# Forming the second round's block sums beside the first output projection, in a two-layer decoder trunk

## The chip, the cores and the metric

The kernel runs on one core of one Trainium2 chip. The metric is the device time of one execution in microseconds (us); a lower time is better. The engines are named as in the profile: PE (matmuls) with PEld (its weight loads), DVE (vector), ACT (activations), POOL (general) and SP, the queue from which this kernel issues its DMAs.

## The reference

Two layers over one sequence of 2048 rows with 1024 columns, all in float32. Layer 0 is called even in the code, layer 1 odd. Only this much bears on the change:

```
def even_layer(x, g_norm, w_in, b_f, g_q, g_k, w_out):
    h = rmsnorm(x, g_norm)
    proj = h @ w_in
    ...
    return x + mixed @ w_out

def odd_layer(x, g_norm, w_in, g_q, g_k, w_out):
    h = rmsnorm(x, g_norm)
    proj = h @ w_in
    q, k, v, gate = jnp.split(proj, split_points(ODD_SIZES), axis=-1)
    ...
    return x + mixed @ w_out
```

The input projection of the odd layer multiplies 2048 x 1024 by 1024 x 5120. Its left operand is the normalised output of the even layer, which comes out of the even layer's output projection.

## The kernel before, in words

**Products by seven.** Each input projection is done in two rounds of 1024 rows. In a round the left operand is cut into two by two blocks of 512 rows by 512 columns, 11 12 over 21 22, and each panel of 512 weight columns is computed with seven block products instead of eight. The left operands are four blocks taken as they are or as sums: A11, A12, S1 = 21 + 22, S2 = S1 - 11, S3 = 11 - 21, A22 = 22, S4 = 12 - S2. The weights' sums are formed the same way by `Weights.prepare` (POOL's line L226 does the sums, then ACT L81 and POOL or DVE L86 split each into a rounded part and a rest). Every product is three matmuls of the rounded parts and rests (`mm3`, L91 to L93), so one block product is 48 matmuls of 128x256, and a panel 336. `panel_steps` runs a panel in the order of `ORDER`; `two` opens two panels at once, with A11 and A12 of both ahead of S2, S3, S1, A22 and S4 of each. DVE adds the partial results (L300) and ACT copies them (L305).

**Where the left operands come from.** In the odd layer `left` makes them. The transposed, normalised rows lie in a DRAM scratch `T` (`hT` in the profile). `left` loads pieces of 128x512 (`lp`, L362), forms the sums on DVE and POOL (helper `tt`, L345) and splits each into its two parts (`put`: ACT L81, DVE L86) into one of eight large buffers. For the first round (`staged=True`) blocks 11 and 12 are loaded once into a buffer `stage`, and the pieces take six small buffers (tags `ld`, `q`, `pT`, two each). For the second round (`staged=False`) no room is left for `stage`: the blocks 11 and 12 are rebuilt from the two parts of the operands already made, and the pieces share the four buffers of tag `c` with other work. Here are the sums that this costs:

```
            for h in half(A[A11], kk):
                tt(s, s, h, sub)
...
            hi, lo = half(A[A12], kk)
            h2, l2 = half(A[S2], kk)
            tt(s, hi, h2, sub)
            tt(s, s, lo, plus)
            tt(s, s, l2, sub)
```

In the even layer the second round is prepared otherwise: `combined_to` makes all seven blocks ahead of time, 128 rows at a time, into a scratch `U`, and `left_ready` only loads and splits.

**The order of the work.** `first_out` is the even layer's output projection: 16 tiles of 128 rows (`rows`), staggered, so that in step s tile s is loaded, tile s-1 multiplied, added to x, stored and normalised, and tile s-2 transposed (L142) and stored to `T`. In steps 13 and 14 it also starts `left` for the first round. Then come the odd layer's panels: first round q and k of group 1 through `two`, then v, then the other groups, then the gate panel. While the gate panel runs, a call after each of its seven products (`after=lambda j: next(nxt)`) moves the second round's `left` one step on, since each product frees one large buffer. Attention units run between the panels' half products. The program is written in this order, but a scheduler may move instructions ahead on an engine when they are ready; each engine and the SP queue then run their instructions strictly in the order they got. All DMAs that matter here are on SP.

Of the kernel before, what the change touches and what calls it, by code (L numbers as in the profile page):

```python
# [8 lines left out]
F32 = mybir.dt.float32  # L9
# [3 lines left out]
OP = mybir.AluOpType  # L13
# [4 lines left out]
P = 128  # L18
S = 2048
D = 1024  # L20
KT = D // P
CH = 512
# [14 lines left out]
class K:  # L37
# [114 lines left out]

    def transpose_to(self, T, src, t, gain):

# [6 lines left out]
        self.transposed(x, gain, lambda z: self.c2([P, 4, P], name="te"),  # L161
                        lambda z, d: nc.sync.dma_start(T[:, z * 4:(z + 1) * 4, t * P:(t + 1) * P], d))

# [12 lines left out]
A11, A12, S2, S3, S1, A22, S4 = range(7)  # L176
# [164 lines left out]

def left(k, T, r, A, staged=True):

# [15 lines left out]
    def piece(block, kk):  # L359
        c = k.c2(name="lp", tag=next(tags))  # L360
        t0 = r * ROUND + block * CH
        nc.sync.dma_start(c, T[:, kk, t0:t0 + CH])  # L362
        return c
# [94 lines left out]
def left_ready(k, U, A, tags):  # L458

    A.extend([None] * 7)  # L460
    tags = itertools.cycle(tags)
    for j in FIRST:
        t = A[j] = k.big([P, 4, 2, CH], F32R, name=f"A{j}")
        for kk in range(4):
            c = k.c2(name="lp", tag=next(tags))
            k.nc.sync.dma_start(c, U[:, j, kk])
            k.split(t[:, kk, 0], t[:, kk, 1], c, "act", "dve")
        yield
# [525 lines left out]
        tail()  # L994


def first_out(k, x, x1, w, T, W, lefts):

    nc = k.nc
    wo, raws, ml = {}, {}, {}
    quarters = [(n, z) for n in range(2) for z in range(2)]

    def load(i):
        n, z = quarters[i]
        raws[i] = [k.raws.tile([P, 2, CH], F32, name="wraw", tag="raw") for _ in range(2)]
        for j, raw in enumerate(raws[i]):  # L1010
            k0 = (z * 4 + j * 2) * P
            nc.sync.dma_start(raw, w[k0:k0 + 2 * P, n * CH:(n + 1) * CH].rearrange("(k p) n -> p k n", p=P))

    def quarter(i):
        t = wo[quarters[i]] = k.big([P, 4, 2, CH], F32R, name="wo")
        for j, raw in enumerate(raws.pop(i)):
            k.split(t[:, 2 * j:2 * j + 2, 0], t[:, 2 * j:2 * j + 2, 1], raw, "act", "dve")

    def mixed(b):
        t = ml[b] = k.big([P, KT, 2, 2 * P], F32R, name="ml")  # L1020
        for j in range(4):
            c = k.c2([P, 2, 2 * P], name="mp", tag="res")
            nc.sync.dma_start(c, k.mixT[:, 2 * j:2 * j + 2, b * 2 * P:(b + 1) * 2 * P])
            k.split(t[:, 2 * j:2 * j + 2, 0], t[:, 2 * j:2 * j + 2, 1], c, "act", "dve")

    def rows(t):
        xt = k.w4([P, D], name="xt")
        nc.sync.dma_start(xt, x[t * P:(t + 1) * P, :])
        yield
        m, i = ml[t // 2], slice(t % 2 * P, (t % 2 + 1) * P)  # L1030
        for n in range(2):
            acc = k.ps("s")
            for kk in range(KT):
                k.mm3(acc, [m[:, kk, z, i] for z in range(2)],
                      [wo[n, kk // 4][:, kk % 4, z] for z in range(2)], kk == 0, kk == KT - 1)
            half = xt[:, n * CH:(n + 1) * CH]
            nc.vector.tensor_tensor(half, acc, half, op=OP.add)
        nc.sync.dma_start(x1[t * P:(t + 1) * P, :], xt)
        k.normalise(xt)
        yield  # L1040
        k.transposed(xt, k.go, lambda z: k.c2([P, 4, P], name="te"),
                     lambda z, d: nc.sync.dma_start(T[:, z * 4:(z + 1) * 4, t * P:(t + 1) * P], d))

    load(0)
    load(1)
    for i in range(4):
        yield
        quarter(i)
        if i < 2:
            load(i + 2)  # L1050
    steps = staggered(rows(t) for t in range(NTT))
    for b in range(2):
        yield
        mixed(b)
    yield
    for s in range(NTT + 2):
        next(steps, None)

        if s in (2, 4, 6, 8, 10, 12):
            mixed(s // 2 + 1)  # L1060
        if s == 9:
            W.ahead(1)
        if s in (13, 14):
            next(lefts)


def odd_layer(k, x, x1, even_w_out, w_in, w_out, out):
    tc, nc = k.tc, k.nc
    c2, dr = k.c2, k.dram
    T = dr.tile([P, KT, S], F32, name="hT1")  # L1070
    plain = lambda c0: [[(c0, 256)], [(c0 + 256, 256)]]
    rounds = [[(n, g) for g in gs for n in "qkv"] + [("gate", 0)] for gs in ((1, 0, 2), (2, 1, 0))]
    cols = lambda n, g: plain(3 * 1536 if n == "gate" else "qkv".index(n) * 1536 + g * 512)
    W = Weights(k, [(w_in, cols(*j)) for js in rounds for j in js], [2, 1, 1, 1, 1, 1, 1, 1, 1] * 2)
    A = []
    lefts = left(k, T, 0, A)
    yield from first_out(k, x, x1, even_w_out, T, W, lefts)
    tick = Pace()
    tick.add(lefts)

# [195 lines left out]

    for r in range(2):
        B = []
        nxt = left(k, T, 1, B, False)
        for i, (name, grp) in enumerate(rounds[r]):  # L1280
            rate = 3 if r == 0 or i < 3 else 1.3
            count = [0.0]

            def beat():
                tick()
                count[0] += 1
                if count[0] >= rate:
                    count[0] -= rate
                    step()

            last = r == 0 and name == "gate"
            if i < 2:
                if i == 0:
                    both = two(A, [emitter(r, *rounds[r][n]) for n in range(2)], beat)
                    next(both)
                    if r == 0:
                        tick.finish()

                        box = k.big([P, 4, HG, 2, P], F32R, name="box")
                        bias = box[:, 0].bitcast(F32)  # L1300
                        values = [box[:, 3].bitcast(F32).rearrange("p a b c -> p (a b c)")[:, i * HW:(i + 1) * HW] for i in range(4)]
                        values += [k.hs.tile([P, HW], F32, name=f"v{i}") for i in range(2)]
                        ring = box[:, 1:3].rearrange("p x a b c -> p (x a b c)").rearrange("p (z h s t) -> p z h s t", z=2, h=2, s=4)
                        pairs = box[:, 1:3].rearrange("p x a b c -> p (x a b c)").rearrange("p (z s h e t) -> p z s h e t", z=2, s=2, h=2, e=2)
                next(both)
            else:
                panel(k, A, W, "t", emitter(r, name, grp), beat, (lambda j: next(nxt)) if last else None)
            if name == "v":
                nblk = S // GROUPS[grp][1] // P
                if nblk == 1:  # L1310
                    if r == 1:
                        queue.extend((True, attention(grp, hf, range(16), range(1))) for hf in range(2))
                else:
                    ns = range(r * nblk // 2, (r + 1) * nblk // 2)
                    queue.extend((False, attention(grp, hf, range(GROUPS[grp][1]), ns)) for hf in range(2))
        A = B
    ws = []
    for n in range(2):
        t = k.big([P, 4, 2, CH], F32R, name="wof")
# [120 lines left out]
```

## Time and profile before

| what | value |
|---|---|
| median of 3 runs | 2769.3 us (2765.4 to 2769.72) |
| the profiled execution | 2767.75 us, of which its span 2766.0 us |
| mean granted PE clock | 0.991 |
| busy: PE, PEld, DVE, ACT, POOL | 96%, 87%, 70%, 57%, 40% of the span |
| first output projection, last tile's matmuls end | about 1477 us |
| first round of the odd layer begins | 1475 us |
| second round of the odd layer begins | 1986 us |

How to read it: matmuls overlap, so a busy PE is not yet a PE at its pace. Better is to count matmuls in a stretch and to compare with a stretch that runs undisturbed; the views by window give both, and the clock that was granted. Lines are those of the kernel before.

### The profile page before, as it was taken

To read this page: it belongs to the slowest core of one execution; us is meant where nothing else is said; L and a number is where in the kernel's file an instruction comes from. 1 tells how busy PE (TensorE), PEld (TensorE's weight loads), DVE (VectorE), ACT (ScalarE), POOL (GpSimd) and SP (SyncE) were. 2 spreads that over 40 slices of the span, in tenths; PEclk is the share of its full clock that TensorE was granted. 3 is DMA by queue.
4 is the path that set the end of the run, shared out by engine and by line. 5 is a ranking of instruction groups with operands and counts; after the bars stand their busy time and mean duration, and the time that the engine had idled before them with its cause. 6 is when DMAs were issued, how large, how long until landed. Compare 5 with 4: busy or idle time off the path is not lost.

```text
span 2766.0 us, 54039 instructions
## 1 busy us (share of the span) xinstructions
PE 2664.9 (96%) x19615; PEld 2418.7 (87%) x19615; DVE 1923.3 (70%) x4255; ACT 1577.2 (57%) x3843; POOL 1102.5 (40%) x903
## 2 busy tenths in 40 slices
PE   6999999999998899999999899999989999999998
PEld 5899878998787789988889899999889999999876
DVE  7867774684788887787237767475896676663976
ACT  6456654454767665665546345555663678665642
POOL 3545654544544433332004654343254432422322
PEclk9999999999999999999999999999999999999999
DMA  5576864445433334443564333444634444444675
GB/s 184 179 214 186 276 209 146 153 143 190 151 115 117 118 116 145 142 132 111 193 203 149 111 108 116 131 133 128 203 98 143 129 154 146 141 138 141 222 257 184
DMA packets 382154, 432.56 MB, mean 156 GB/s; under 512 B 30976, under 2 KB 315968, under 8 KB 381888
## 3 DMA queue, kind: packets, MB, share of 16 engines
q1 hardware_dynamic: 381888, 429.11, 48.3%
q8 instruction: 155, 2.54, 0.4%
q14 instruction: 111, 0.91, 0.1%
HBM read 271.30 MB, written 157.71 MB: 155 GB/s over the span
## 4 chain that ended last, share of the span: by engine, by line
PE 70%; DVE 17%; ACT 5%; DMA 3%; issue 3%; POOL 1%; SPq 1%; DVEq 0%; ACTq 0%; POOLq 0%
PE ps L91 19%; PE ps L93 19%; PE ps L92 19%; DVE rest L893 4%; PE ps L928 3%; PE ps L1237 2%; PE ps L1227 2%; PE ps L1208 2%; PE ps L1153 1%; DVE pT L86 1%; DVE wop L86 1%; DVE c L300 1%; DVE row L1214 1%; PE ps L1200 1%; DVE lp L345 1%
## 5 line engine op out<-in xcount | busy, mean ns | idle before, releaser
L226 POOL TENSOR_TENSOR wraw<-wraw 128x512 f32<-128x512 f32 (+1 forms) x288 | 396.7, 1388 | 417.2 <-DVE wop L86 158.0
L91 PE MATMUL ps<-wop,A 128*128 128x256 f32 (+1 forms) x1856 | 528.5, 285 | 3.8 <-DVE c L300 3.8
L92 PE MATMUL ps<-wop,A 128*128 128x256 f32 (+1 forms) x1856 | 527.2, 284 | 0.0
L93 PE MATMUL ps<-wop,A 128*128 128x256 f32 (+1 forms) x1856 | 525.5, 283 | 0.0
L81 ACT ACTIVATE wop<-wraw 128x512 fp32r<-128x512 f32 (+1 forms) x504 | 315.4, 628 | 339.6 <-PE ps L93 266.0
L86 POOL TENSOR_TENSOR wop<-wraw,wop 128x512 fp32r<-128x512 f32 (+1 forms) x216 | 291.2, 1351 | 494.4 <-ACT wop L81 479.5
L86 DVE TENSOR_TENSOR wop<-wraw,wop 128x512 fp32r<-128x512 f32 (+1 forms) x288 | 234.1, 814 | 239.8 <-ACT wop L81 237.6
L91 PE MATMUL ps<-wop,S 128*128 128x256 f32 x1280 | 369.8, 289 | 4.5 <-DVE c L300 4.5
L92 PE MATMUL ps<-wop,S 128*128 128x256 f32 x1280 | 364.1, 284 | 2.4 <-DVE wop L86 2.4
L93 PE MATMUL ps<-wop,S 128*128 128x256 f32 x1280 | 365.6, 286 | 0.0
L91 PEld LDWEIGHTS ps<-wop,A 128*128 128x128 f32 x1856 | 351.9, 190 | 8.1 <-DVE c L300 4.6
L93 PEld LDWEIGHTS ps<-wop,A 128*128 128x128 f32 x1856 | 352.3, 190 | 1.2 <-issue 0.7
L92 PEld LDWEIGHTS ps<-wop,A 128*128 128x128 f32 x1856 | 352.0, 190 | 0.7 <-issue 0.5
L91 PEld LDWEIGHTS ps<-wop,S 128*128 128x128 f32 x1280 | 242.6, 190 | 8.8 <-issue 8.0
L92 PEld LDWEIGHTS ps<-wop,S 128*128 128x128 f32 x1280 | 243.1, 190 | 4.2 <-DVE wop L86 2.6
L93 PEld LDWEIGHTS ps<-wop,S 128*128 128x128 f32 x1280 | 242.8, 190 | 3.4 <-issue 2.7
L81 ACT ACTIVATE pT<-ps 128x512 fp32r<-128x512 f32 (+2 forms) x352 | 164.7, 502 | 136.8 <-PE ps L928 93.4
L300 DVE TENSOR_TENSOR c<-u,ps 128x512 f32<-128x512 f32 (+1 forms) x242 | 157.4, 656 | 90.3 <-PE ps L93 84.6
L86 DVE TENSOR_TENSOR pT<-ps,pT 128x512 fp32r<-128x512 f32 (+2 forms) x352 | 187.7, 559 | 43.8 <-ACT pT L81 42.3
L896 POOL TENSOR_TENSOR rows<-rows,rest 128x512 f32<-128x512 f32 (+4 forms) x160 | 152.4, 956 | 160.3 <-DVE rest L893 153.1
L1220 ACT ACTIVATE row<-row,nm 128x256 f32<-128x256 f32 (+1 forms) x384 | 172.4, 451 | 64.2 <-DVE nm L1218 60.6
L93 PE MATMUL ps<-A,wop 128*128 128x512 f32 x448 | 177.2, 397 | 4.4 <-DVE ms L104 4.4
(222 smaller groups left out, 6778.3 us busy)
## 6 DMA issues: line engine op xcount, KB each, us to landing
wraw<-in_odd_w_in_dram SPq DMA_DIRECT2D x88, 512.0 KB, 4.0
wraw<-in_even_w_in_dram SPq DMA_DIRECT2D x70, 512.0 KB, 4.2
ld<-qk SPq DMA_DIRECT2D x106, 256.0 KB, 3.1
qk<-c SPq DMA_DIRECT2D x96, 256.0 KB, 2.5
uu<-ot SPq DMA_DIRECT2D x96, 132.0 KB, 1.9
fin<-uu SPq DMA_DIRECT2D x16, 792.0 KB, 4.7
xt<-in_x_dram SPq DMA_DIRECT2D x24, 512.0 KB, 4.5
vv<-c SPq DMA_DIRECT2D x48, 256.0 KB, 2.5
```

The source lines that it names most:

```text
L81: nc.scalar.activation(hi, src, AF.Copy)
L86: (nc.vector if lo_on == "dve" else nc.gpsimd).tensor_tensor(lo, src, hi.bitcast(F32), op=OP.subtract)
L91: mm(out, a[0], b[0], start=start, stop=False, skip_group_check=more)
L92: mm(out, a[0], b[1], start=False, stop=False, skip_group_check=more)
L93: mm(out, a[1], b[0], start=False, stop=stop, skip_group_check=more)
L226: tt = lambda e, o, x, y, op, s: e.tensor_tensor(o[:, s], x[:, s], y[:, s], op=op)
L300: nc.vector.tensor_tensor(out[g], x[g], y[g], op=OP.add)
L893: nc.vector.tensor_tensor_scan(o[:, b:b + n][:, ::-1], back, k.ident[:, :1].to_broadcast([P, n]), 1.0 if carry is None else carry, OP.mult ...
L896: nc.gpsimd.tensor_tensor(dst[:, :w], dst[:, :w], o[:, b + 1:b + 1 + w], op=OP.mult)
L928: nc.tensor.transpose(pt[:, (jx * 2 + i) * P:(jx * 2 + i + 1) * P], rows[:, i, (jj * 2 + jx) * P:(jj * 2 + jx + 1) * P], k.ident)
L1208: nc.tensor.matmul(scores(hp, e), q[pr, za, hp], ring[pr, zb, hp, blocks], start=i == 0, stop=i == 2)
L1220: nc.scalar.activation(row[:, h // 2, h % 2, :nk], row[:, h // 2, h % 2, :nk], AF.Exp, bias=nm[:, h:h + 1], accum_out=ot[:, HW + HG + h:HW ...
```

## The change

The second round's seven blocks are no longer made from `T` during the gate panel. They are made in `first_out`, as the even layer does it, from the tiles as they are transposed: tiles 8 to 11 hold the upper blocks 11 and 12 and go to the new scratch `U` as they are. For each tile 12 to 15 the matching upper blocks are loaded back (`above`, two DMAs, tag `res`), and A22, S1, S2, S3 and S4 are formed and stored: two operations on POOL, two on DVE, five stores. In the gate panel `left_ready` loads and splits what lies in `U`. `T` shrinks to the first round's rows. The first round still uses `left` with `stage`, in the same steps 13 and 14.

```
@@ first_out, rows(t)
         xt = k.w4([P, D], name="xt")
         nc.sync.dma_start(xt, x[t * P:(t + 1) * P, :])
+        at = slice(t % 4 * P, (t % 4 + 1) * P)
+        if t >= 12:
+            a = [k.c2([P, 4, P], name="above", tag="res") for _ in range(2)]
+            for z in range(2):
+                nc.sync.dma_start(a[z], U[:, (A11, A12)[z], :, at])
         yield
...
-        k.transposed(xt, k.go, lambda z: k.c2([P, 4, P], name="te"),
-                     lambda z, d: nc.sync.dma_start(T[:, z * 4:(z + 1) * 4, t * P:(t + 1) * P], d))
+        if t < 8:
+            k.transposed(xt, k.go, lambda z: k.c2([P, 4, P], name="te"),
+                         lambda z, d: nc.sync.dma_start(T[:, z * 4:(z + 1) * 4, t * P:(t + 1) * P], d))
+            return
+
+        def store(j, d):
+            nc.sync.dma_start(U[:, j, :, at], d)
+
+        if t < 12:
+            k.transposed(xt, k.go, lambda z: k.c2([P, 4, P], name="te"), lambda z, d: store((A11, A12)[z], d))
+            return
+        b = [k.c2([P, 4, P], name="te") for _ in range(2)]
+        k.transposed(xt, k.go, lambda z: b[z])
+        store(A22, b[1])
+        s1, s2, s4 = (k.c2([P, 4, P], name="lp", tag=n) for n in ("ld", "q", "pT"))
+        nc.gpsimd.tensor_tensor(s1, b[0], b[1], op=OP.add)
+        store(S1, s1)
+        nc.vector.tensor_tensor(s2, s1, a[0], op=OP.subtract)
+        store(S2, s2)
+        nc.gpsimd.tensor_tensor(b[0], a[0], b[0], op=OP.subtract)
+        store(S3, b[0])
+        nc.vector.tensor_tensor(s4, a[1], s2, op=OP.subtract)
+        store(S4, s4)
@@ odd_layer
-    T = dr.tile([P, KT, S], F32, name="hT1")
+    T = dr.tile([P, KT, S // 2], F32, name="hT1")
+    U = dr.tile([P, 7, 4, CH], F32, name="hU1")
...
-        nxt = left(k, T, 1, B, False)
+        nxt = left_ready(k, U, B, ("c",))
```

The tiles `s1`, `s2` and `s4` take the buffers of tags `ld`, `q` and `pT`, which the first round's pieces `lp` take as well. So the scheduler places the first round's work anew. The instructions of all engines keep their order elsewhere; they move in two places: from the last tiles of `first_out` into the first two panels, and beside the gate panel.

**The SP queue at the end of `first_out`.** Before, a piece is `lp<-hT`, the transposed rows `hT<-te`, a panel's weights `wraw`, the first results `qk<-c`:

```order
L1038 DMA x1d<-xt 128x1024
L1042 DMA hT_7557<-te 128x4x128 x2
L362 DMA lp<-hT_7557 128x512 x5
L1038 DMA x1d<-xt 128x1024
L362 DMA lp<-hT_7557 128x512
L1042 DMA hT_7557<-te 128x4x128
L1134 DMA box<-biases 128x1024
L1042 DMA hT_7557<-te 128x4x128
L216 DMA wraw<-in_odd_w_in_dram 128x4x256 x2
L1042 DMA hT_7557<-te 128x4x128 x2
L216 DMA wraw<-in_odd_w_in_dram 128x4x256
L1121 DMA qk_16985<-c 128x2x256 x2
```

These were the last six of the sixteen pieces. In the changed kernel the same place, from the last store of tile 14 on, reads as follows (L1054 is a store to `U`; `te` is a transposed tile or S3, `lp` one of S1, S2, S4):

```order
L216 DMA wraw<-in_odd_w_in_dram 128x4x256
L1054 DMA hU_7558<-te 128x4x128
L362 DMA lp<-hT_7557 128x512
L1054 DMA hU_7558<-lp 128x4x128
L362 DMA lp<-hT_7557 128x512
L1054 DMA hU_7558<-lp 128x4x128
L362 DMA lp<-hT_7557 128x512
L1054 DMA hU_7558<-lp 128x4x128
L362 DMA lp<-hT_7557 128x512
L216 DMA wraw<-in_odd_w_in_dram 128x4x256
L362 DMA lp<-hT_7557 128x512
L1054 DMA hU_7558<-te 128x4x128
```

All sixteen pieces now stand behind the transposed tile 15, the first of them directly behind its A22 store; the seventh to ninth stand behind the first results `qk<-c`, and the last four behind all results of both opened panels' first products.

**DVE at the same place.** Before, the splits of S2 (`S_17027`), S3 (`S_17095`), S1 (`S_17164`) stand between the last two tiles' additions (L1037):

```order
L112 TENSOR_SCALAR t<-t 128x1
L86 TENSOR_TENSOR S_17027<-lp,S_17027 128x512
L114 TENSOR_TENSOR r_16844<-r,t 128x1
L86 TENSOR_TENSOR S_17027<-lp,S_17027 128x512 x2
L1037 TENSOR_TENSOR xt<-ps,xt 128x512
L86 TENSOR_TENSOR S_17027<-lp,S_17027 128x512
L86 TENSOR_TENSOR S_17095<-stage,S_17095 128x512 x4
L345 TENSOR_TENSOR lp<-lp 128x512
L86 TENSOR_TENSOR S_17164<-lp,S_17164 128x512 x2
L1037 TENSOR_TENSOR xt<-ps,xt 128x512
```

In the changed kernel they come after the first normalised result (L1146, which was L1117), and S2 (`S_17084`) and S3 (`S_17152`) are made slice by slice between the panels' own work:

```order
L1146 TENSOR_TENSOR c<-c,r_17280 128x512 x2
L345 TENSOR_TENSOR lp<-lp 128x512
L86 TENSOR_TENSOR wop<-wraw,wop 128x2x256
L345 TENSOR_TENSOR lp<-lp,stage 128x512
L345 TENSOR_TENSOR stage<-stage,lp 128x512
L300 TENSOR_TENSOR c<-u,ps 128x512
L86 TENSOR_TENSOR S_17084<-lp,S_17084 128x512
L300 TENSOR_TENSOR c<-u,ps 128x512
L86 TENSOR_TENSOR S_17152<-stage,S_17152 128x512
L124 TENSOR_REDUCE ss<-sq 128x8
L345 TENSOR_TENSOR lp<-lp,stage 128x512
```

All forming and splitting of S2, S3, S1, A22 and S4 moved from ahead of the last tile's addition to behind the first opened panel's first result. The fourth slice of S2 is split 22 rows after the first, the fourth of S1 another 17 rows on.

**DVE beside the end of the gate panel.** Before, at S4 of the second round (`S_23812`; `A_23154` is A12, `S_23296` is S2; L1109 and L1113 belong to the gate's results):

```order
L1109 TENSOR_SCALAR e<-c 128x512
L345 TENSOR_TENSOR lp<-A_23154,S_23296 128x512
L345 TENSOR_TENSOR lp<-lp,A_23154 128x512
L345 TENSOR_TENSOR lp<-lp,S_23296 128x512
L1113 TENSOR_TENSOR c<-c,e 128x512
L345 TENSOR_TENSOR lp<-A_23154,S_23296 128x512
L345 TENSOR_TENSOR lp<-lp,A_23154 128x512
L86 TENSOR_TENSOR S_23700<-lp,S_23700 128x512
L86 TENSOR_TENSOR S_23812<-lp,S_23812 128x512
L345 TENSOR_TENSOR lp<-lp,S_23296 128x512
L86 TENSOR_TENSOR wop<-wraw,wop 128x2x256
L345 TENSOR_TENSOR lp<-A_23154,S_23296 128x512
```

In the changed kernel, at S4 (`A_23837`; `A_23746` is A22, L1138 and L1142 are the gate's lines):

```order
L300 TENSOR_TENSOR c<-u_23006,ps 128x512 x2
L86 TENSOR_TENSOR A_23746<-lp,A_23746 128x512 x2
L86 TENSOR_TENSOR wop<-wraw,wop 128x2x256
L1142 TENSOR_TENSOR c<-c,e 128x512
L86 TENSOR_TENSOR A_23837<-lp,A_23837 128x512
L1142 TENSOR_TENSOR c<-c,e 128x512
L86 TENSOR_TENSOR A_23837<-lp,A_23837 128x512
L1138 TENSOR_SCALAR e<-c 128x512 x2
L86 TENSOR_TENSOR wop<-wraw,wop 128x2x256
```

Only the splits are left; the L345 rows are gone.

More of the change, by code (lines that the diff above doesn't have):

```diff
@@ L994, in even_attention, with first_out @@
         tail()
-def first_out(k, x, x1, w, T, W, lefts):
+def first_out(k, x, x1, w, T, U, W, lefts):
     nc = k.nc
@@ L1076, in odd_layer @@
     lefts = left(k, T, 0, A)
-    yield from first_out(k, x, x1, even_w_out, T, W, lefts)
+    yield from first_out(k, x, x1, even_w_out, T, U, W, lefts)
     tick = Pace()
```

## The prediction

> **What bounds the kernel now.** First the page: is PE the bound, and of what whole?
>
> ```profile
> span 2766.0 us, 54039 instructions
> PE 2664.9 (96%) x19615; PEld 2418.7 (87%) x19615; DVE 1923.3 (70%) x4255; ACT 1577.2 (57%) x3843; POOL 1102.5 (40%) x903
> ```
>
> PE is busy 96% of the span, so a saving elsewhere counts only where PE waits. The change touches two places, the beginning of the first and of the second round of the odd layer, so next come the windows there. The first row below is an ordinary panel of 336 matmuls with its attention units, as a yardstick; then four stretches from the start of the first round (both panels' A11 and A12; S2, S3, S1 of the first panel; its A22 and S4; S2, S3, S1 of the second); then four from the gate panel on (gate panel; A11 and A12 of both panels; S2, S3, S1 of the first; A22, S4 and the second's S2, S3, S1). The columns are the stretch, its length, busy time and count by engine, the granted clock, DMA.
>
> ```profile
> core 0: us, PE busy (x) PEld busy (x) DVE busy (x) ACT busy (x) POOL busy (x), PEclk, DMA share, GB/s
> 1702.25:1756.01 53.76, 53.76 (x483) 50.75 (x482) 32.06 (x83) 28.46 (x80) 18.07 (x15) 1.00 0.44 139
> ...
> 1475.08:1500.67 25.59, 24.64 (x209) 24.44 (x208) 18.56 (x30) 19.91 (x48) 14.27 (x11) 1.00 0.49 144
> 1500.67:1517.74 17.07, 17.07 (x147) 17.07 (x145) 15.24 (x24) 5.40 (x11) 10.25 (x8) 1.00 0.38 124
> 1517.74:1529.20 11.46, 11.46 (x98) 11.35 (x96) 4.74 (x10) 3.16 (x7) 6.05 (x5) 1.00 0.37 116
> 1529.20:1555.91 26.71, 19.76 (x146) 19.31 (x145) 21.80 (x34) 7.72 (x16) 18.94 (x14) 0.87 0.31 104
> ...
> 1928.82:1985.84 57.02, 55.70 (x495) 51.83 (x493) 44.81 (x99) 37.22 (x91) 16.14 (x12) 1.00 0.60 188
> 1985.84:2028.23 42.39, 33.30 (x263) 31.02 (x261) 37.12 (x59) 25.56 (x59) 21.91 (x14) 0.88 0.40 128
> 2028.23:2054.38 26.15, 26.01 (x239) 23.98 (x237) 24.76 (x57) 19.11 (x54) 10.19 (x9) 1.00 0.39 127
> 2054.38:2095.16 40.78, 39.54 (x358) 37.12 (x357) 32.55 (x70) 22.18 (x59) 21.28 (x16) 1.00 0.39 126
> ```
>
> The ordinary panel does 483 matmuls in 53.76 us, 8.98 per us. At that pace the 495+263+239+358 = 1355 matmuls from 1928.82 on take 150.8 us; they took 166.34. So **15.5 us are lost around the second round's start**, 13.1 of them in the second row (263/8.98 = 29.3 against 42.39), where DVE is busy 37.12 of 42.39. In the first round 147 matmuls take 17.07 us without attention (8.61 per us); by this the last stretch, 26.71 us, has lost 9.8 (146/8.61 = 17.0), and the ones ahead of it nothing.
>
> Who makes PE wait in the 42.39 us, and what DVE does there:
>
> ```profile
> PE ps L91 <- DVE c L300: 3.6, 2, 2.6
> PE ps L1227 <- ACT uT L1241: 3.1, 1, 3.1
> ...
> L345 DVE TENSOR_TENSOR lp<-lp,A 128x512 f32<-128x512 f32 x16 | 15.1, 941 | 3.6 <-POOL lp L345 3.4
> L86 DVE TENSOR_TENSOR S<-lp,S 128x512 fp32r<-128x512 f32 x15 | 11.9, 805 | 0.0
> L86 DVE TENSOR_TENSOR A<-lp,A 128x512 fp32r<-128x512 f32 x12 | 9.8, 860 | 5.1 <-ACT A L81 5.1
> L345 DVE TENSOR_TENSOR lp<-A,S 128x512 f32<-128x512 f32 x4 | 3.8, 954 | 0.0
> L345 DVE TENSOR_TENSOR lp<-lp,S 128x512 f32<-128x512 f32 x4 | 3.7, 924 | 0.0
> L345 DVE TENSOR_TENSOR lp<-A,lp 128x512 f32<-128x512 f32 x4 | 2.7, 687 | 0.7 <-DMA lp<-hT 0.7
> L345 DVE TENSOR_TENSOR lp<-lp 128x512 f32<-128x512 f32 x4 | 2.7, 685 | 0.6 <-DMA lp<-hT 0.6
> ```
>
> PE's longest waits are for L300, which stands in DVE's queue behind the second round's sums, and for ACT's attention work that the same backlog holds up.
>
> **What goes.** The five L345 groups: 16+4+4+4+4 = 32 instructions, 15.1+3.8+3.7+2.7+2.7 = 28.0 us of DVE; and four POOL sums. The 28 loads and 28 splits stay. DVE in the gate panel and the stretch after it then has 44.81+37.12-28.0 = 53.9 us to do in 55.1+29.3 = 84.4 us at the ordinary pace, 64%; the ordinary panel has 32.06 of 53.76, 60%. So PE's loss should mostly vanish. What is late next is the SP queue:
>
> ```profile
> 1988.98 5.89 SPq L362 DMA_DIRECT2D lp<-hT  x2
> ...
> 382.03 0.47 PE L91 MATMUL ps<-A,wop 128*128 128x512 f32 x1 [0.32 <-DVE c L300]
> ```
>
> Two loads of pieces held the queue 5.89 us, with the next weights behind them; the same loads of `U` can be held by the same four buffers. Against that stands the even layer, where `left_ready` already does this step: 0.32 us is the largest wait of PE there (second row), though without attention units. Bounds of the gain: 6 (only half of the 13.1 comes back) to 15.5; I take **13**, nearer to the even layer's row, with 2.5 left for the queue.
>
> **What is added in `first_out`.** Eight DVE and eight POOL operations, eight loads, and 28 stores in the place of 16. Tiles 12 and 13 have them beside the output projection's matmuls; I count them nothing there: DVE's idle time in the groups below shows the room. The loads of `above` for tiles 14 and 15 wait on SP until tiles 12 and 13 have used their buffers, and behind them stand the stores of `x1`, which must have read a tile before it is normalised in place. A tile's two POOL and two DVE operations are 2 x 1.42 + 2 x 0.69 = 4.2 us (rows below), which PE's next tile covers; uncovered they would cost that much. Those of tiles 14 and 15 are in the chain below.
>
> **What moves.** This is the dear part. The first round's pieces of S2, S3, S1, A22 and S4 are made between 1395 and 1500 now:
>
> ```profile
> L86 DVE TENSOR_TENSOR S<-lp,S 128x512 fp32r<-128x512 f32 x8 | 6.4, 827 | 0.0
> L86 DVE TENSOR_TENSOR S<-stage,S 128x512 fp32r<-128x512 f32 x8 | 5.0, 687 | 0.0
> L345 DVE TENSOR_TENSOR lp<-lp 128x512 f32<-128x512 f32 x4 | 2.8, 693 | 10.7 <-DMA lp<-hT 10.7
> L345 DVE TENSOR_TENSOR lp<-lp,stage 128x512 f32<-128x512 f32 x4 | 2.6, 689 | 6.1 <-POOL lp L345 3.1 <-DMA stage<-hT 3.0
> L86 DVE TENSOR_TENSOR A<-lp,A 128x512 fp32r<-128x512 f32 x4 | 2.6, 687 | 0.3 <-ACT A L81 0.3
> L345 DVE TENSOR_TENSOR stage<-stage,lp 128x512 f32<-128x512 f32 x2 | 1.4, 680 | 0.0
> ...
> L345 POOL TENSOR_TENSOR stage<-stage,lp 128x512 f32<-128x512 f32 x6 | 9.2, 1558 | 37.1 <-DVE A L86 36.2 <-DVE lp L345 0.9
> L226 POOL TENSOR_TENSOR wraw<-wraw 128x512 f32<-128x512 f32 x7 | 9.2, 1341 | 1.4 <-DVE ms L104 0.7 <-DMA wraw<-in_odd_w_in_dram 0.7
> L345 POOL TENSOR_TENSOR lp<-lp 128x512 f32<-128x512 f32 x4 | 5.7, 1422 | 119.8 <-DMA lp<-hT 119.8
> ...
> L149 ACT ACTIVATE te<-ps,go x128: 343/376/410, 1316.5 to 1496.0; 128x128 f32<-128x128 f32 x128
> ...
> L362 SPq DMA_DIRECT2D lp<-hT x16: 319/332/681, 1399.6 to 1478.6; - x16
> lp<-hT SPq DMA_DIRECT2D x44, 256.0 KB, 3.6
> ```
>
> 6.4+5.0+2.8+2.6+2.6+1.4 = 20.8 us of DVE and 14.9 of POOL, now hidden beside the output projection, go behind the last tile in the new order. PE wants S2 at 1500.67. I follow the queue. Tile 15's transposes stand 89 matmuls into the first products: 1475.1 + 89/8.61 + 2.3 for tile 14's and its own transposes (24.64 less 192/8.61, first row of the round) gives 1487.7; eight ACT copies of 0.376 give `te` near 1490.5. Its first sum waits on POOL behind three weight sums (1.3 each), so it is done near 1495; only then does SP let the second piece go, which lands 3.6 later, 1499. DVE's sum stands behind the first normalised result, about 1501; two subtractions, the split by ACT and DVE: the first slice of S2 at **1505 to 1507**. PE idles 5 to 6 us. The fourth slice is 22 rows later on DVE, some of them waiting for the second panel's statistics and POOL: at 0.7 each 15 us, beside POOL more, so 1522 to 1527. The fourth of S1 is 17 rows on, 12 us: 1535 to 1539. After it PE still has 38 matmuls of S1 and A22 and 48 of S4: 10 us, so the first panel ends at 1545 to 1549 instead of 1529.20. The second panel's three products then need 17.1 us: 1562 to 1566 against 1555.91, a loss of 6 to 10, since the old wait of 9.8 lies in that stretch already:
>
> ```profile
> 1517.44 0.33 SPq L1143 DMA_DIRECT2D ld<-qk  x1
> ...
> 1542.49 0.55 PE L91 MATMUL ps<-wop,S 128*128 128x256 f32 x1 [4.34 <-DVE c L300]
> ```
>
> Those weights stood behind `ld<-qk` on SP, and now arrive while PE still waits for operands. But the second row's kind of wait, DVE late with L300, may come again with more in DVE's queue: up to 4 more. Bounds 0 (all of it within the old wait) to 24 (below); I take **10**.
>
> **Sum.** 2767.75 (the profiled execution: span 2766.0 and 1.75 around it) - 13 + 10 = 2764.75. The median of the runs, 2769.3, is 1.55 above that execution, which gives 2766.3; I say **2765**. Likeliest case: gain 11 to 15.5, loss 6 to 14, so 2758 to 2771.
>
> The Trainium skill, "TensorE: Matmul & The Clock Gate", section "Why this matters for your kernels", warns of PE gaps over about 3 us, after which the array runs at half clock. The granted clock of 0.87 in the row at 1529.20, which holds the 4.34 us wait, and 0.88 in the row at 1985.84 agree. By the rule the new gap at 1500 costs a slow spell of its own, about 12% of 26 us as in these rows, an estimate of 3 us: 2768.
>
> **Rivals.**
> 1. *The late operands cost nothing net.* The second panel's old wait of 9.8 us takes up the whole delay; the loss is 0 to 3. For it: the weights come early now. Against: DVE's 20.8 us are real work. 2767.75 - 13 + 2 = 2756.75, **2757**.
> 2. *Slower: DVE and POOL hold each other up.* DVE's operations from two buffers take 0.68 us alone and 1.65 to 1.77 beside POOL's weight sums:
>
> ```profile
> 2016.71 0.68 DVE L345 TENSOR_TENSOR lp<-lp,S 128x512 f32<-128x512 f32 x1
> ...
> 2025.55 1.77 DVE L345 TENSOR_TENSOR lp<-lp,A 128x512 f32<-128x512 f32 x1
> ...
> 2019.90 6.87 POOL L226 TENSOR_TENSOR wraw<-wraw 128x512 f32<-128x512 f32 x4 [6.91 <-DMA wraw<-in_odd_w_in_dram]
> ```
>
> In the new order 28 POOL operations lie between the last tile's first weight sum and the fourth slice of S1. If half of them hold up a DVE operation by 1.0 us that the chain waits for, 14 us come on top of 10: a loss of 24, 2767.75 - 13 + 24 = **2779**. It decides once the loss passes 19, that is once the second panel's S1 ends after 1575. The Trainium skill, "SBUF — State Buffer", section "Who interferes with whom", says that a DVE instruction with two SBUF inputs and a GpSimd one that reads SBUF exclude each other. The rows agree, and it speaks against this change.
> 3. *The gate panel stays slow*: the queue's wait of 5.89, or the gate's stores, hold it instead. Gain 6, loss 10: 2767.75 + 4 = **2772**.
>
> **How the numbers follow.** About 0.2%, 5.5 us, is what a measurement of this kernel can tell from no change, so faster means under 2763.8 and slower over 2774.8. The forecast gets 0.5 (0.2 of it faster, 0.3 within), rival 1 0.2 (faster), rival 2 0.2 (slower), rival 3 0.1 (within). Faster 0.4, same 0.4, slower 0.2. The range reaches from below rival 1 to near rival 2: 2754 to 2778.
>
> **What would show it.** Right: the gate panel in about 55 us, the first four products of the second round in 29 to 32 with clock 1.00 and no L345; a PE gap of 5 to 6 us near 1500 for S2's split and the second panel's S1 ending at 1562 to 1570, everything after it shifted alike. Wrong: no gap at 1500, or an end there past 1575; or PE still waiting for L300 at 1990 to 2025 with DVE under 70%.

## The result, and the profile after

The changed kernel takes 2784.53 us (median of 4 runs, 2782.71 to 2790.86), beside 2768.78 for the kernel before. The ratio is 1.0063, 95% interval 1.0051 to 1.0075: it is slower by 0.63%, 15.75 us by the medians. The forecast was 2765, so sign and range both missed. The profiled execution took 2784.53 us:

```profile
span 2782.8 us, 54078 instructions
PE 2666.9 (96%) x19615; PEld 2419.9 (87%) x19615; DVE 1907.2 (69%) x4231; ACT 1577.4 (57%) x3843; POOL 1111.8 (40%) x907
```

DVE has less to do than before (1907.2 against 1923.3 us), and PE's busy time is 2 us longer, yet the span grew by 16.8. The time went into one place and came out of another. The windows of the changed kernel show both. The first three rows are the first round: A11 and A12 of both panels; S2, S3, S1, A22 of the first panel; its S4 with S2, S3, S1 of the second. The last row is the gate panel.

```profile
core 0: us, PE busy (x) PEld busy (x) DVE busy (x) ACT busy (x) POOL busy (x), PEclk, DMA share, GB/s
1478.20:1509.53 31.33, 24.12 (x204) 23.71 (x202) 21.10 (x28) 14.85 (x37) 20.68 (x14) 0.94 0.65 201
1509.53:1556.28 46.75, 32.61 (x193) 29.57 (x194) 40.14 (x51) 17.75 (x33) 32.52 (x21) 0.75 0.37 121
1556.28:1589.60 33.32, 25.48 (x198) 25.27 (x197) 27.05 (x38) 9.77 (x22) 17.66 (x13) 0.85 0.29 95
1961.69:2016.78 55.09, 55.09 (x494) 51.74 (x493) 40.03 (x94) 44.13 (x108) 14.12 (x10) 1.00 0.68 215
```

The same two stretches of the kernel before, and its 109 us behind the gate panel in one row, for comparison:

```profile
1500.67:1523.47 22.80, 22.80 (x194) 22.80 (x193) 18.41 (x32) 7.29 (x15) 10.58 (x9) 1.00 0.46 149
1523.47:1555.91 32.44, 25.49 (x195) 24.93 (x193) 23.37 (x35) 8.99 (x18) 24.67 (x18) 0.89 0.26 87
1985.84:2095.16 109.32, 98.85 (x854) 92.13 (x853) 94.43 (x184) 66.86 (x171) 53.38 (x37) 0.95 0.39 127
```

And the changed kernel behind its gate panel:

```profile
2016.78:2112.00 95.22, 94.38 (x846) 88.45 (x845) 68.88 (x157) 58.91 (x152) 48.06 (x35) 1.00 0.41 135
```

- **Gain.** The gate panel lost 1.9 us of its length (57.02 to 55.09), and 846 matmuls behind it take 95.22 us at clock 1.00 where 854 took 109.32. The first 262 of these take 29.22 us; 263 took 42.39 before. In all, the changed kernel is 32.9 us late when the gate panel starts (1961.69 against 1928.82) and 16.8 late at the end of the span: **16.1 us won**.
- **Loss.** The second panel's S1 ends at 1589.60 instead of 1555.91: **33.7 us lost**. The start is 3.1 late (1478.20 against 1475.08). A11 and A12 take 5.7 more. S2 to A22 take 46.75 instead of 22.80, which is 24.0: about 14 us in which PE is not busy, and 9.8 because 193 matmuls keep it busy for 32.61 us, at clock 0.75, where 194 took 22.80. The last stretch adds 0.9. The 3.1 at the start need not be the change's: the round starts at 1474.5 in late_alone (below), which has the same sums, and at 1477.6 in later_pool, whose output projection is as before.

What PE waited for in the first round of the changed kernel (waits as engine, line and releaser: total, times, longest; then the longest one's row):

```profile
PE ps L91 <- DVE u L300: 10.8, 3, 7.8
PE ps L91 <- ACT S L81: 9.8, 4, 6.3
PE ps L93 <- DVE S L86: 7.7, 6, 3.9
...
1576.12 0.55 PE L91 MATMUL ps<-wop,S 128*128 128x256 f32 x1 [7.84 <-DVE u L300]
```

The two rows on `S` are operands that come late, as forecast. The row on L300 is not: it is DVE behind with the panels' own additions. DVE's timeline in the changed kernel shows why. These are the statistics (L110 to L114, 128x16), a normalised result (L1146), a weight split, and the addition PE waits for; then two of POOL's rows beside them:

```profile
1561.51 1.26 DVE L111 TENSOR_TENSOR t<-t,ms 128x16 f32<-128x16 f32 x1
1562.81 1.22 DVE L112 TENSOR_SCALAR t<-t 128x16 f32<-128x16 f32 x1
1564.06 1.21 DVE L114 TENSOR_TENSOR r<-r,t 128x16 f32<-128x16 f32 x1
...
1565.30 3.48 DVE L1146 TENSOR_TENSOR c<-c,r 128x512 f32<-128x512 f32 x2
1568.70 1.23 DVE L111 TENSOR_TENSOR t<-t,ms 128x16 f32<-128x16 f32 x1
...
1573.62 1.75 DVE L86 TENSOR_TENSOR wop<-wraw,wop 128x512 fp32r<-128x512 f32 x1
1575.29 1.27 DVE L300 TENSOR_TENSOR u<-u,ps 128x512 f32<-128x512 f32 x2
```

```profile
1561.46 2.53 POOL L226 TENSOR_TENSOR wraw<-wraw 128x512 f32<-128x512 f32 x2 [4.31 <-DVE ss L124]
...
1573.18 3.32 POOL L1148 TENSOR_TENSOR c<-c,oq 128x512 f32<-128x512 f32 x2 [0.84 <-DVE c L1146]
```

Most operations on 16 columns take 1.2 us here, and 0.17 from 1586 to 1590, where POOL is idle. POOL was at weight sums (L226) and splits (L86) until 1569.9, and then at work on the results (L1148). DVE's operations from 1561.51 to 1575.29 took about 9.5 us more in all than the same operations undisturbed in this kernel (0.17, 0.68, and 1.29 for the pair), so being held up is enough to make a wait of 7.84.

### The profile page after: what moved, and what is told of

Read it like the earlier page. It is cut to its first block, busy times and chain, and to the rows that moved or that the text cites. A ratio compares the mean times of both kernels' runs of the same rounds, so it can differ in the third digit from the quotient of the medians.

```text
span 2782.8 us, 54078 instructions
## 1 busy us (share of the span) xinstructions
PE 2666.9 (96%) x19615; PEld 2419.9 (87%) x19615; DVE 1907.2 (69%) x4231; ACT 1577.4 (57%) x3843; POOL 1111.8 (40%) x907
## 5 line engine op out<-in xcount | busy, mean ns | idle before, releaser
L91 PE MATMUL ps<-wop,A 128*128 128x256 f32 (+1 forms) x2496 | 711.8, 285 | 1.1 <-DVE c L300 1.0
L92 PE MATMUL ps<-wop,A 128*128 128x256 f32 (+1 forms) x2496 | 708.9, 284 | 0.9 <-POOL wop L86 0.9
L93 PE MATMUL ps<-wop,A 128*128 128x256 f32 (+1 forms) x2496 | 707.9, 284 | 0.0
L226 POOL TENSOR_TENSOR wraw<-wraw 128x512 f32<-128x512 f32 (+1 forms) x288 | 396.3, 1387 | 409.8 <-DVE wop L86 153.6
L86 POOL TENSOR_TENSOR wop<-wraw,wop 128x512 fp32r<-128x512 f32 (+1 forms) x216 | 292.4, 1356 | 507.7 <-ACT wop L81 497.0
L91 PEld LDWEIGHTS ps<-wop,A 128*128 128x128 f32 x2496 | 471.4, 189 | 6.5 <-issue 4.3
L92 PEld LDWEIGHTS ps<-wop,A 128*128 128x128 f32 x2496 | 471.7, 189 | 3.3 <-issue 1.4
L93 PEld LDWEIGHTS ps<-wop,A 128*128 128x128 f32 x2496 | 471.3, 189 | 2.2 <-issue 1.0
L86 DVE TENSOR_TENSOR wop<-wraw,wop 128x512 fp32r<-128x512 f32 (+1 forms) x288 | 232.6, 809 | 237.5 <-ACT wop L81 232.3
L300 DVE TENSOR_TENSOR c<-u,ps 128x512 f32<-128x512 f32 (+1 forms) x242 | 157.6, 656 | 98.8 <-PE ps L93 94.8
L86 DVE TENSOR_TENSOR pT<-ps,pT 128x512 fp32r<-128x512 f32 (+2 forms) x352 | 187.8, 560 | 45.2 <-ACT pT L81 43.7
L91 PE MATMUL ps<-wop,S 128*128 128x256 f32 x640 | 188.0, 294 | 20.6 <-DVE u L300 10.8
L93 PE MATMUL ps<-wop,S 128*128 128x256 f32 x640 | 184.0, 291 | 7.8 <-DVE S L86 7.7
L92 PE MATMUL ps<-wop,S 128*128 128x256 f32 x640 | 183.0, 286 | 0.0
L93 PE MATMUL ps<-A,wop 128*128 128x512 f32 x448 | 177.2, 397 | 4.7 <-DVE wop L86 4.7
L92 PE MATMUL ps<-A,wop 128*128 128x512 f32 x448 | 177.5, 396 | 2.0 <-DVE A L86 2.0
L92 PE MATMUL ps<-pT,vt 128*128 128x256 f32 x576 | 171.6, 300 | 7.6 <-DVE pT L86 5.9
L91 PE MATMUL ps<-A,wop 128*128 128x512 f32 x448 | 178.0, 398 | 0.0
```

The source lines that it names most:

```text
L86: (nc.vector if lo_on == "dve" else nc.gpsimd).tensor_tensor(lo, src, hi.bitcast(F32), op=OP.subtract)
L91: mm(out, a[0], b[0], start=start, stop=False, skip_group_check=more)
L92: mm(out, a[0], b[1], start=False, stop=False, skip_group_check=more)
L93: mm(out, a[1], b[0], start=False, stop=stop, skip_group_check=more)
L226: tt = lambda e, o, x, y, op, s: e.tensor_tensor(o[:, s], x[:, s], y[:, s], op=op)
L300: nc.vector.tensor_tensor(out[g], x[g], y[g], op=OP.add)
```

## The experiments

All times are medians, each beside runs of the kernel before on the same chip. "S1 ends" is the start of the product behind the second panel's S1 in PE's timeline (1555.9 in the kernel before, 1589.6 in the changed one); it comes from the one profiled execution of each kernel.

### The two halves of the change, apart

**own_place.** The changed kernel, with the sums in other buffers:

```diff
-        s1, s2, s4 = (k.c2([P, 4, P], name="lp", tag=n) for n in ("ld", "q", "pT"))
+        s1 = k.c2([P, 4, P], name="lp")
...
-        nc.vector.tensor_tensor(s2, s1, a[0], op=OP.subtract)
-        nc.vector.tensor_tensor(s4, a[1], s2, op=OP.subtract)
+        nc.vector.tensor_tensor(a[0], s1, a[0], op=OP.subtract)
+        nc.vector.tensor_tensor(a[1], a[1], a[0], op=OP.subtract)
```

> The changed kernel, but the sums of tiles 12 to 15 take no buffers of the tags ld, q and pT: S2 and S4 are formed in the buffers of above, S1 in one of te's. All loads, sums and stores of the change stay. Theory A (the loss comes only from the first round's pieces being queued behind tile 15, because they share those buffers): S2 is split beside the output projection again, the second panel's S1 ends at 1556 to 1560 as before, the 16 us at the second round's start stay won, 2750 to 2756 us. Theory B (the added sums, loads and stores themselves cost the time): the second panel's S1 still ends past 1575, 2775 to 2785 us.

**buffers_alone.** The kernel before, with one edit in the transposes of `rows`:

```diff
-lambda z: k.c2([P, 4, P], name="te"),
+lambda z: k.c2([P, 4, P], name="te", tag=("ld", "q")[z] if t >= 12 else "c"),
```

> The kernel before, with one edit: the transposed tiles te of tiles 12 to 15 take the buffers of the tags ld and q. No sum, load or store is added. Theory A: the first round's pieces wait behind tile 15 as in the changed kernel, the second panel's S1 ends at 1580 to 1592, and as the second round is formed as before nothing is won back: 2793 to 2803 us. Theory B: 2766 to 2772 us. If the delay is worth only the 10 us that were forecast, and the rest comes from the added work: 2778 us.

**sums_alone** (own_place) and **late_alone** (the changed kernel), both with the second round as before and all rows kept in `T`:

```diff
-        nxt = left_ready(k, U, B, ("c",))
+        nxt = left(k, T, 1, B, False)
```

> The sums of tiles 12 to 15 are formed and stored as in own_place, in no shared buffer, but the second round still forms its operands from the transposed rows as before (those are stored as well: 12 stores more than the changed kernel has, counting both). So the sums are added and nothing is won. Theory A: the added work is hidden, 2766 to 2772 us. Theory B: 2785 to 2800 us.

> The changed kernel with its sums in the shared buffers, but the second round still forms its operands from the transposed rows as before. Loss and gain come apart: if the gain at the second round's start is the 16 us read from the two traces, 2784.5 + 16 = 2800 us (2797 to 2804). Should the gate panel's shorter time have another cause than the operands formed early, 2784 us.

They have 16 stores more than the changed kernel, not 12 as the expectation says.

| kernel | us | ratio to before, 95% interval | S1 ends |
|---|---|---|---|
| own_place | 2765.88 | 0.9985 (0.9976 to 0.9994) | 1567.0 |
| buffers_alone | 2794.54 | 1.0094 (1.0080 to 1.0108) | 1579.7 |
| sums_alone | 2783.30 | 1.0052 (1.0038 to 1.0066) | 1568.7 |
| late_alone | 2803.23 | 1.0126 (1.0111 to 1.0142) | 1585.7 |

Theory A, that only the shared buffers cost time, was half right. The kernel before was at 2768.53, so the buffers alone cost 26 us, with nothing computed in addition. The sums alone cost 14.8 with no shared buffer, which theory A put at nothing. Together they cost 34.7, less than the sum of 40.8. The gain is the difference of two pairs: sums_alone less own_place 17.4, late_alone less the changed kernel 18.7. In both pairs the slower kernel also carries the 16 additional stores, so part of the 14.8, and of the 1 to 3 us by which the pairs exceed the 16.1 of the traces, may be theirs. Theory B, that the added work costs all of it, fell by buffers_alone. own_place and sums_alone came out between the ranges of the two theories, as two causes would have it; late_alone came out in the range for the gain.

What the sums hold up shows in the queue of SP (SyncE) at tile 14 in own_place (the start, the time the entry held the queue, line, transfer):

```profile
1487.31 0.43 SPq L1054 DMA_DIRECT2D hU<-te  x1
1491.70 0.37 SPq L1054 DMA_DIRECT2D hU<-lp  x1
1493.40 0.36 SPq L1054 DMA_DIRECT2D hU<-te  x1
1493.86 0.45 SPq L216 DMA_DIRECT2D wraw<-in_odd_w_in_dram  x1
1495.20 2.70 SPq L1054 DMA_DIRECT2D hU<-above  x2
1497.99 0.46 SPq L216 DMA_DIRECT2D wraw<-in_odd_w_in_dram  x1
```

Before, both weight loads stood together:

```profile
1486.87 3.85 SPq L216 DMA_DIRECT2D wraw<-in_odd_w_in_dram  x2
```

The first of the two now goes out 7 us later, and the second 11, after stores that wait for POOL's and DVE's sums. PE itself waits for no weights in own_place up to that S1; if late ones cost time, it is through DVE, where their splits stand ahead of L300. It waits 3.9 us for tile 15's normalised row (0.9 before), whose statistics (L110) stand on DVE behind a subtraction that waited for POOL (L1067), and 4.5 for `u L300`:

```profile
1493.40 1.77 DVE L1067 TENSOR_TENSOR above<-lp,above 128x512 f32<-128x512 f32 x1 [1.18 <-POOL te L1065]
...
1496.76 0.15 DVE L110 TENSOR_TENSOR t<-r 128x1 f32<-128x1 f32 x1
...
1499.20 1.94 PE L142 MATMUL ps<-ident,xt 128*128 128x128 f32 x8 [3.94 <-ACT xt L133]
```

### What in the sums costs it

**later.** `first_out` and `T` as before the change. A generator loads slices of `T`, forms the sums and stores them to `U`; the sixth panel steps it. `left_ready` takes A11, A12 and A22 from `T`:

```diff
+            a, b, b2, a2 = piece(0, 0), piece(1, 0), piece(1, 1), piece(0, 1)
+            nc.gpsimd.tensor_tensor(b2, b, b2, op=OP.add)
+            nc.gpsimd.tensor_tensor(b, a, b, op=OP.subtract)
+            nc.vector.tensor_tensor(a, b2, a, op=OP.subtract)
+            nc.vector.tensor_tensor(a2, a2, a, op=OP.subtract)
...
+(lambda j: next(sums, None)) if r == 0 and i == 5
```

> The first output projection exactly as before the change. The same sixteen sums for the second round are formed one panel in the middle of the first round (beside its sixth panel, with attention units) from loaded slices of the transposed rows, and stored; the second round loads ready operands as in the changed kernel. If the added sums cost 15 us only because of their place at the start of the first round: the second panel's S1 ends at 1556 to 1560 as before, the 17 us at the second round's start stay won, 2749 to 2757 us. If eight additions on VectorE and eight on GpSimd with 32 transfers cost the same wherever they stand: 2764 to 2772 us.

**later_pool.** The two `nc.vector` of later become `nc.gpsimd`.

> later with all sixteen sums on GpSimd. In later the panel with the sums lost 6.5 us and the two after it 1.6 each; VectorE sat idle 4.3 us there ahead of a sum that waited for GpSimd, with the attention's work behind it. If that wait in VectorE's queue is the cost: the panel takes 54 to 55 us as before the change and the kernel 2754 to 2759 us. If the transfers or GpSimd's additions cost it: 2764 to 2769 us, as in later.

**sums_no_store** is sums_alone without the 20 stores to `U` of tiles 12 to 15; **stores_no_sum** is sums_alone without the sums and the loads of `above`, with `te` stored in their places.

> sums_alone without the 20 stores of A22, S1, S2, S3 and S4: the sums of tiles 12 to 15 are formed and thrown away, the loads of above stay. sums_alone was 14.8 us above the kernel before. If the operations on VectorE and GpSimd cost it (they hold up each other and the rows of tile 15 and the panels' own additions behind them): 2778 to 2784 us. If the stores, which wait in SyncE's queue for the sums with the next weights behind them, cost it: 2767 to 2773 us.

> sums_alone without the sums and without the loads of above: the transposed tiles themselves are stored 20 times in the places of A22, S1, S2, S3 and S4; the second round does not read them. If the operations cost the time: 2767 to 2772 us. If the number of transfers does: 2778 to 2784 us. If only stores that wait for sums in SyncE's queue do: 2767 to 2773 us here and also in sums_no_store.

**own_pool** and **own_dve** are own_place with all `nc.vector` of the sums as `nc.gpsimd`, and the reverse.

> own_place with all four sums of a tile on GpSimd, none on VectorE. own_place took 2765.9 us. If it is VectorE's longer queue that costs the time: 2757 to 2762 us. If GpSimd's additions, which slow VectorE's operations beside them and stand ahead of the weights' sums, cost it: 2768 to 2776 us.

> own_place with all four sums of a tile on VectorE, none on GpSimd. own_pool took 2761.8 us, own_place 2765.9. If VectorE's queue is what costs the time: 2768 to 2772 us. If it is the mixture, sums that wait for the other engine on both: 2761 to 2765 us.

| kernel | us | ratio to before, 95% interval | S1 ends |
|---|---|---|---|
| sums_no_store | 2779.16 | 1.0041 (1.0028 to 1.0054) | 1565.2 |
| stores_no_sum | 2773.90 | 1.0018 (1.0008 to 1.0028) | 1560.4 |
| own_pool | 2761.76 | 0.9974 (0.9964 to 0.9984) | 1563.7 |
| own_dve | 2760.79 | 0.9970 (0.9959 to 0.9981) | 1561.0 |
| later | 2766.03 | 0.9986 (0.9977 to 0.9995) | 1556.8 |
| later_pool | 2759.69 | 0.9964 (0.9952 to 0.9977) | 1557.9 |

The operations without stores cost 0.41%, the stores without operations 0.18% (28 stores more than in the kernel before, where the changed kernel has 12 more), both 0.52%: two shares, the larger one the operations'. sums_no_store came out in the range for the operations, stores_no_sum between its two. With the sums on one engine, whichever, the kernel is 3 to 4 us quicker by the ratios than with both. The intervals overlap, so this is likely rather than settled. own_pool lies in the range that blamed DVE's longer queue, but own_dve, with the longest queue on DVE, is no slower; that fits sums which wait for the other engine in two queues.

later came out in its second range, but not for the reason given there, since later_pool with the same sums and transfers does better. The first round is whole again (1556.8), and the place with the sums pays. This is a stretch of seven products with the first half of the sums, and the same stretch in later_pool:

```profile
1677.80:1738.20 60.40, 56.94 (x484) 53.40 (x481) 44.74 (x102) 30.46 (x87) 24.14 (x18) 0.94 0.54 171
```

```profile
1678.70:1734.30 55.60, 54.19 (x483) 50.89 (x481) 41.26 (x98) 30.39 (x87) 24.43 (x19) 1.00 0.52 161
```

The stretch took 53.9 before the change. In later two of the sums stand on DVE ahead of the attention's row maxima (L1215), and PE waits for these:

```profile
1722.01 0.69 DVE L1291 TENSOR_TENSOR lp<-lp 128x512 f32<-128x512 f32 x1
1722.72 1.63 DVE L1293 TENSOR_TENSOR lp<-lp 128x512 f32<-128x512 f32 x1
...
1725.16 1.11 PE L1228 MATMUL ps<-ident,row 128*128 128x128 f32 x4 [3.46 <-DVE ot L1215]
```

In later_pool this wait is 1.30 us. The 4.3 us for which a sum on DVE waited for POOL, named in later_pool's expectation, come later, at 1761.87, outside this stretch. On POOL alone the stretch is back at 55.6 (54 to 55 expected), with the same transfers and more additions on POOL, and the kernel just above its first range. By its median later_pool is the fastest kernel here that does the whole work, 0.36% below the kernel before; own_dve's interval overlaps with its.

### Why the delay was 26 us and not 10

**buffers_dve.** buffers_alone, with the `left` sums of the first round on VectorE:

```diff
-(e or nc.vector).tensor_tensor(o, a, b, op=op)
+(e if e and not staged else nc.vector).tensor_tensor(o, a, b, op=op)
```

> buffers_alone (2794.5 us) with the ten sums of the first round's operands that GpSimd makes (L345) on VectorE instead. If GpSimd's sums hold up VectorE's operations beside them, and the waits between the two engines make up the part of the delay that the forecast missed: 2780 to 2789 us. If VectorE's long queue alone sets when the operands come: its ten more operations of 0.7 us make it 2797 to 2803 us.

It took 2793.62 us, ratio 1.0088 (1.0074 to 1.0102), S1 ends at 1579.9: neither range. Moving ten operations from POOL to DVE left the time where it was; whether two effects cancel or neither matters, the run doesn't tell.

**after_bare** and **before_bare** have this edit in `Weights.prepare`, with `W.bare = True` for the odd layer. They leave out the weight sums (L226) of the first two panels in the changed kernel and in the kernel before:

```diff
-                    for args in work:
+                    for args in () if getattr(self, "bare", False) and i < 2 else work:
```

> The changed kernel without the sixteen sums of the weights for S2 and S1 of the first two panels (L226 on GpSimd); the products of those two panels then take the weights' blocks unsummed. Nothing is added on VectorE. In the changed kernel PE waits 7.84 us for L300 at 1576, while VectorE's 128x16 operations of the statistics take 1.2 us each beside these sums instead of 0.17. If GpSimd's operations hold VectorE up and this is the part of the delay that the forecast missed: that wait falls under 3 us, the second panel's S1 ends at 1573 to 1581 instead of 1589.6, 2768 to 2776 us. If it is the order of VectorE's queue, whatever runs beside it: 2780 to 2786 us.

> The kernel before, with the same sixteen sums left out. If the 9.8 us that were already lost ahead of the second panel's S1 are VectorE held up by GpSimd: the second panel's S1 ends at 1546 to 1550 instead of 1555.9, 2759 to 2763 us. If they are weights that come late on SyncE's queue, as the forecast read them: 2765 to 2770 us.

after_bare took 2775.61 us, ratio 1.0020 (1.0010 to 1.0030), in the range for DVE held up by POOL; S1 ends at 1565.5, earlier than either theory had it, but in an execution of 2767.91, the fastest of its ten. before_bare took 2758.77, ratio 0.9957 (0.9939 to 0.9974), just under the range for DVE held up; S1 ends at 1546.5, as expected of it. The last stretch (S4, and the second panel's S2, S3, S1) in before_bare and in after_bare:

```profile
1523.70:1546.50 22.80, 22.80 (x194) 22.80 (x193) 17.73 (x32) 8.12 (x17) 14.47 (x10) 1.00 0.36 119
```

```profile
1542.69:1565.49 22.80, 22.80 (x195) 22.80 (x193) 19.03 (x32) 7.69 (x16) 14.51 (x10) 1.00 0.35 116
```

In both, PE no longer waits at all there: 32.44 and 33.32 us become 22.80. DVE's groups in this stretch (count, busy time, mean ns) in before_bare:

```profile
L1118 DVE TENSOR_TENSOR c<-c,r 128x512 f32<-128x512 f32 x6 | 3.9, 685 | 0.0
...
L112 DVE TENSOR_SCALAR t<-t 128x16 f32<-128x16 f32 x2 | 0.3, 170 | 0.0
```

and in the changed kernel:

```profile
L1146 DVE TENSOR_TENSOR c<-c,r 128x512 f32<-128x512 f32 x4 | 4.8, 1234 | 0.0
L124 DVE TENSOR_REDUCE ss<-sq 128x8 f32<-128x512 f32 x5 | 3.4, 677 | 0.7 <-ACT sq L123 0.7
...
L112 DVE TENSOR_SCALAR t<-t 128x16 f32<-128x16 f32 x2 | 2.4, 1198 | 0.1
```

L112, the same instruction, has a mean of 170 ns in before_bare and 1198 in the changed kernel. It depends on what falls beside it: in the kernel before, with the weight sums, L112 keeps 175 ns in this stretch, and the normalised results (L1117 there) take 964. In the changed kernel DVE had no idle time worth the name in this stretch before L300, and in after_bare the wait is gone, so there the wait of 7.84 us is DVE held up by POOL. In the kernel before, DVE also sat idle 8.7 us for weight splits, and the runs don't divide its 9.8 us between that and the holding up: leaving the sums out makes the weights ready earlier as well.

The stretch ahead of it didn't gain: S2 to A22 take 44.48 us in after_bare (1498.21 to 1542.69), against 46.75. Operands that are formed behind the last tile keep PE waiting with or without the weight sums. By the ratios the weight sums cost 0.43% in either kernel, about 12 us. In the profiled execution of after_bare the first round up to that S1 is 20 us shorter than in the changed kernel, but that execution ends only 16.7 us earlier, and the median is 9 us lower; where the rest goes stays open.

## Why the prediction was wrong

- **The gain: right in kind, a little too small.** 13 was forecast (bounds 6 to 15.5), 16.1 read from the traces, 17.4 and 18.7 from the pairs. The gate panel took 55.09 us for "about 55", with no L345. SP's queue, for which 2.5 were kept in reserve, made PE wait nowhere: its waits from 1920 to 2125 sum up to 0.8 us and are the attention's.
- **"Those of tiles 14 and 15 are in the chain below": the first failed step.** The sums of tiles 12 and 13 were counted as nothing, and in the changed kernel they are: PE waits for nothing from 1330 to the round's start (at most 2.2 us in own_place and sums_alone). For tiles 14 and 15, though, the chain contained only the wait for one sum on POOL, done "near 1495" (its store went out at 1496.89). The subtractions and stores, and what stands behind them on DVE and SP, were priced at nothing. In buffers_alone, with shared buffers and without the sums, the first slice of S2 is split at 1498.37; in the changed kernel at 1511.00. The sums cost 8.7 us on top of the shared buffers (late_alone less buffers_alone) and 14.8 by themselves, both with the 16 additional stores. Idle time of an engine was the wrong measure: SP held the next weights behind stores that waited for sums, and DVE held tile 15's row behind a subtraction that waited for POOL.
- **"the old wait of 9.8 lies in that stretch already": the second failed step.** The forecast let it vanish, since weights "now arrive while PE still waits for operands". The weights did come in time, and yet 33.32 us were needed for 22.80 of work: 10.5 lost again. In the changed kernel the wait is DVE's, slowed by POOL, and both bare kernels lose it together with the weight sums. buffers_alone, with no sums added, has it too: PE waits 6.31 us for L300 at 1566.11. Rival 2 named this mechanism, but as 14 us on top of the delay; its 2779 was the nearest of the times forecast.
- **The operands' delay: right in kind, too small.** The first slice of S2 was split at 1511.0, forecast 1505 to 1507; the fourth at 1532.1, forecast 1522 to 1527; the fourth of S1 at 1547.8, forecast 1535 to 1539. In these rows of DVE stands one reason:

```profile
1520.56 1.25 DVE L110 TENSOR_TENSOR t<-r 128x16 f32<-128x16 f32 x1
1521.73 0.68 DVE L345 TENSOR_TENSOR stage<-stage,lp 128x512 f32<-128x512 f32 x1
1522.34 1.25 DVE L111 TENSOR_TENSOR t<-t,ms 128x16 f32<-128x16 f32 x1
1523.50 0.68 DVE L86 TENSOR_TENSOR S<-lp,S 128x512 fp32r<-128x512 f32 x1
1524.11 1.24 DVE L112 TENSOR_SCALAR t<-t 128x16 f32<-128x16 f32 x1
```

  The statistics' small operations were priced like the others or less; each took 1.25 us. Another is the work left behind the last slice of S1: the forecast had 38 matmuls of S1 and A22 there, and from 1549.00 to A22's end there were 64, in 7.28 us. The first panel's A22 ended at 1556.3. The forecast end of that panel, 1545 to 1549, less 5.7 for S4, had it at 1539 to 1543. In buffers_alone it ended at 1548.2, so about 8 of the 13 to 17 us belong to the added sums, and 5 to 9 to the delay itself.
- **The sum.** 6 forecast with 17 of later operands, or 10 with 13, and 10.5 that did not vanish make 33.5; 33.7 was measured.
- **The ends.** "An end there past 1575" was named as a sign of being wrong, as the point at which rival 2 decides; 1589.6 is past it. The range stopped at 2778 because the loss's bound of 24 contained neither the sums of tiles 14 and 15 nor the old wait.
- **The clock.** After a wait of 6.34 us the granted clock fell to 0.75 in the stretch from 1509.53, as the Trainium skill, "TensorE: Matmul & The Clock Gate", section "Why this matters for your kernels", has it for gaps over about 3 us. The prediction's estimate was 3 us; PE was busy 9.8 us longer there for the same matmuls. How much of that late operands would have taken anyway was not isolated; own_place has a cleaner case, below.

## What to carry to other kernels

Work moved into an engine's idle time is free only if nothing urgent stands behind it in any in-order queue it passes: follow its stores and loads through the DMA queue and its cross-engine waits, and try a chain of sums on one engine alone, so that neither waits for the other in its queue (3 to 4 us here, likely rather than settled). Before a new temporary takes a shared buffer tag, look for who takes that tag next in program order: here two shared tags cost 26 us with no work added. And don't let an old wait absorb a new delay until its cause is known; if that cause moves with the work, it is paid again.

## What the hardware showed unexpectedly

Holding up costs small operations most: a 128x16 operation of DVE with 0.17 us of work takes about as long as the POOL operation beside it, 1.2 us, while the reductions (L124) keep their mean of 677 ns in the same stretch and the additions with one operand from PSUM (L300) 0.64 for each of the two in the row at 1575.29. The Trainium skill, "SBUF — State Buffer", section "Who interferes with whom", excludes both kinds from the contention; the rows agree.

In two runs here a single wait of PE is followed by slow matmuls. In own_place PE waits 4.55 us at 1513.27 and then has everything it needs:

```profile
1517.82:1531.65 13.83, 13.83 (x97) 13.83 (x97) 10.06 (x19) 3.48 (x7) 2.98 (x3) 0.81 0.64 198
1531.65:1537.38 5.73, 5.73 (x50) 5.73 (x49) 5.17 (x7) 2.63 (x6) 5.31 (x4) 1.00 0.66 193
```

97 matmuls take 13.83 us at clock 0.81; by the second row's pace (50 in 5.73) they take 11.1. The wait costs 2.7 us more than itself. In sums_no_store a wait of only 1.97 us, with 50 matmuls in 5.83 us at clock 1.00 ahead of it, was followed by the same:

```profile
1518.32:1531.28 12.96, 12.96 (x96) 12.96 (x97) 10.48 (x19) 3.73 (x8) 2.98 (x3) 0.87 0.39 124
```

That is 96 matmuls, 11.0 us by that pace: 2 us lost behind a wait shorter than the 3 us or so that the Trainium skill gives in "TensorE: Matmul & The Clock Gate", section "Why this matters for your kernels"; the measurement decides.
